# GpSimd no longer splits weights, and a list scheduler gets new durations: a two-block transformer on one Trainium2 core

## The chip, the cores and the metric

The kernel runs on one core of one Trainium2 chip. The metric is the device time of one execution in microseconds; three executions are timed, and a profiled one gives the trace.

## The reference

The input is one sequence of 256 tokens of width 1024. Two blocks follow one another, with two layers each, all in float32.

- A layer of the first block is `x + 0.5*rmsnorm(swiglu(rmsnorm(x)))` (hidden width 2816), then `x + rmsnorm(token_mixing(rmsnorm(x)))`, then a second swiglu of the same kind. The mixing holds three kinds of attention (banded with a relative bias, differential, stick-breaking) and an output projection.
- A layer of the second block is `x + merged @ w_out`, where `merged` is a gated sum of three branches (sparse attention over compressed, selected and windowed keys; chunked gated linear attention; attention into 256 memory tokens), then `x + relu(rmsnorm(x) @ w_up)**2 @ w_down` with hidden width 4096.

Two formulas matter below: `rmsnorm(x, g) = x * rsqrt(mean(x*x) + eps) * g`, and the gated linear attention's decay, which the kernel builds by products with a running state (its "scan").

## The kernel before, in words

**Weights.** All weights are cut on the host into 636 "halves" of 128x1024 float32 (512 KB). `loads` brings them in order through SP's DMA queue into 3 raw buffers (`raw`). Each is split into a rounded part and a rest: `splits` writes the first (`hl<-raw`, a cast on ScalarE), and the second is `raw - first` (`hl<-raw,hl`). A matrix product is then three passes on TensorE (first by first, first by rest, rest by first), summed in PSUM. The ring of split weights (`hl`) has 6 places. The rest is computed by `lows` on VectorE, in one 128x1024 piece (two of 128x512 while `rush` is set, in a handover), or by `pooled` on GpSimd, in four pieces of 128x256. `pooled` runs only if `POOLED` is true; it takes the second weight in the line, or in a handover the first.

**Stages.** `ffn1`, `mix`, `ffn2` for layer 0 and 1, then `hyb`, `mlp` for layer 0 and 1. In each, TensorE goes through the weights in order. The 256 tokens are two row tiles, t = 0 and t = 1.

**Handover.** At the end of a stage `finish` does the last products tile by tile, and `residual` and `norm` make the next stage's input: ScalarE squares and sums (`scr<-b`), VectorE multiplies by the gain (`scr<-b,scr`), `rstd` takes the inverse root (VectorE adds, `small<-small`, and GpSimd raises to the power -0.5, `small<-small,mhalf`), VectorE adds to the residual (`x<-scr,small,x`, two of 128x512). Then the same again for the next norm, and `turn_half` scales (`scr<-x,small,scr`, two halves), TensorE transposes (`b<-ident,scr`, four for a half), ScalarE casts (`hT<-b`) and VectorE subtracts (`hT<-b,hT`). `ws_first` then starts the next stage's first weights on the tile that is ready. In the first block "fill" matmuls (`m<-hl,hmem`, keys and values of the memory tokens for the second block, 24 for a weight) stand between these steps on TensorE. `gains` loads the gains by a broadcast DMA to 128 rows and scales them on GpSimd (128x1024).

**Order.** No order is written by hand. Every task (`loads`, `splits`, `lows`, `residual`, ...) is a generator that yields operations, and `Sched.run` emits, again and again, the operation that could start earliest by its own model of the engines (ties by priority; `SLACK` and `YIELD` hold back some background work). The model's durations come from `Engine.make` (VectorE, ScalarE, GpSimd, DMA), `mm` and `tr` (TensorE) and `matmul`, `when`, `issue`, which also decide when an engine is free. So a changed number there moves instructions on all engines. Each engine then works through its list in order and waits on semaphores. Since `issue` emits everything, nearly all rows of the trace have its line, L546.

A slot given to the ring or the raw buffers is reused in order:

```
            for o in range(0, 1024, 256):
                s = slice(o, o + 256)
                yield self.nc.gpsimd.tensor_sub(t[:, 1, s], raw[:, s], t[:, 0, s].bitcast(FT))
            self.raws.put(raw)
```

In the scan of a `hyb` stage GpSimd multiplies by constants (`scr<-scr,tC` of 128x128, 128x256 and 128x512), and TensorE then takes the results in small products (`b<-scr,scr`). GpSimd also does the powers of the head norms (`sts<-sts,mhalf`, 128x16 for the queries of the sparse attention).

Of the kernel before, what the change touches and what calls it, by code (L numbers as in the profile page):

```python
# [302 lines left out]
class Op:  # L303

    __slots__ = ("eng", "call", "args", "kw", "cost", "tail", "outs", "ins", "tab", "rdy", "stamp", "fn", "load",
                 "passes", "cols", "dep", "name")

    def __init__(self, eng, call, args, kw, cost, outs, ins, tail=0.0, tab=None, fn=None, load=0.0, passes=1, cols=0.0):
        self.eng, self.call, self.args, self.kw, self.cost, self.tail, self.tab = eng, call, args, kw, cost, tail, tab
        self.load, self.passes, self.cols = load, passes, cols  # L310
        self.outs = [r for r in map(region, outs) if r]
        self.ins = [r for r in map(region, ins) if r]
        self.rdy = self.stamp = self.dep = self.name = None
        self.fn = fn

# [31 lines left out]
class Engine:  # L347
# [5 lines left out]
    def __getattr__(self, fn):  # L353
# [3 lines left out]
        def make(*args, **kw):  # L357
# [8 lines left out]
            if "dma" in fn:  # L366
                size = max(_free(a) for a in aps if a.space != bass.MemoryType.DRAM) * 4 * 128
                return Op(e, real, args, kw, size / 360e3, outs, ins, 1.8, fn=fn)
            ps = any(a.space == bass.MemoryType.PSUM for a in outs + ins)
# [10 lines left out]
            else:  # L380
                k, b = 2.07, 0.157
                if kw.get("op") == OP.pow:
                    k, b = 167.0, 0.3
                elif fn == "tensor_scalar":
                    k, b = 0.85, 0.24 if ptr else 0.15
                elif fn == "tensor_copy":
                    k = 3.4
                elif fn == "memset":
                    k, b = 1.0, 0.0
# [17 lines left out]
class Sched:  # L407
# [5 lines left out]
    def __init__(self):  # L413
        self.t = {}
        self.acc = {}
        self.ver = {}
        self.table = None
        self.tasks = []
# [67 lines left out]
    def stream(self, s, cost, cols):  # L486
# [10 lines left out]
        return s  # L497

    def matmul(self, op):
        w = self.ready(op)  # L500
        for i in range(op.passes):
            ld = max(self.loader, w) + op.load
            self.loader = max(ld, self.t.get("pe", 0.0) + 0.002)
            if i == 0:
# [4 lines left out]
    def when(self, op):  # L509
        c = self.t.get(op.eng, 0.0)  # L510
        if op.eng == "pe":
            return max(c, max(self.loader, self.ready(op)) + op.load)
        s = max(c, self.ready(op))
        if op.tab and self.table not in op.tab and op.fn:
            s += 1.28 if op.eng == "act" else 0.0
        return s

    def issue(self, t):
# [5 lines left out]
        if op.eng == "sp":  # L524
            self.t["sp"] = s + 0.06
            d = max(self.t.get("dma", 0.0), s)
# [5 lines left out]
        else:  # L532
            e = s + op.cost
            self.t[op.eng] = e
        for regs, w in ((op.ins, False), (op.outs, True)):
            for n, ps, p0, p1, lo, hi in regs:
# [10 lines left out]
        if self.log is not None and r is not None:  # L547
            op.name = getattr(getattr(r, "ins", r), "name", None)
            self.log.append((op.name, op.eng, op.fn, s, e, op.cost, op.rdy, op.dep and op.dep.name, op.dep and op.dep.eng, t.gen.__name__))
        self.step(t)  # L550
# [58 lines left out]
class Prog:  # L609
# [52 lines left out]
    def mm(self, out, lhsT, rhs, start, stop, **kw):  # L662
        n, m = _free(rhs), _free(lhsT)
        wide = 2 if rhs.dtype == FT else 1
        return Op("pe", self.nc.tensor.matmul, (out,), dict(lhsT=lhsT, rhs=rhs, start=start, stop=stop, **kw),
                  wide * 0.4167e-3 * n, [out], [lhsT, rhs], fn="mm", load=0.836e-3 * m, passes=wide,
                  cols=wide * n * rhs.shape[0] / 128)

    def tr(self, out, in_, k=128):
        i = self.ident[:k, :k]  # L670
        return Op("pe", self.nc.tensor.transpose, (out, in_, i), {}, 0.8333e-3 * k, [out], [in_, i], fn="tr", load=0.107, cols=2 * k)

# [71 lines left out]

    POOLED = True
    rush = False
# [1451 lines left out]
```

## Time and profile before

| | us |
|---|---|
| median of 3 executions | 2017.01 |
| lowest, highest | 2014.21, 2018.1 |
| the profiled execution's own time | 2013.92 |
| its span, first to last instruction | 2012.0 |
| TensorE (PE) busy | 1963.7 (98%) |
| VectorE (DVE) busy | 1424.6 (71%) |
| ScalarE (ACT) busy | 1203.0 (60%) |
| GpSimd (POOL) busy | 267.9 (13%) |

The span is a little shorter than the time, which also holds what lies before the first and after the last instruction. Busy means that an instruction of the engine was under way; matmuls are pipelined, so a busy TensorE need not be at its peak. The granted clock (PEclk, a share of 2.4 GHz) has the mean 0.993 over the span. PEld is TensorE's weight load, which runs beside its matmuls.

### The profile page before, as it was taken

To read this page: it belongs to the slowest core of one execution; us is meant where nothing else is said; L and a number is where in the kernel's file an instruction comes from. 1 tells how busy PE (TensorE), PEld (TensorE's weight loads), DVE (VectorE), ACT (ScalarE), POOL (GpSimd) and SP (SyncE) were. 2 spreads that over 40 slices of the span, in tenths; PEclk is the share of its full clock that TensorE was granted. 3 is DMA by queue.
4 is the path that set the end of the run, shared out by engine and by line. 5 is a ranking of instruction groups with operands and counts; after the bars stand their busy time and mean duration, and the time that the engine had idled before them with its cause. 6 is when DMAs were issued, how large, how long until landed. Compare 5 with 4: busy or idle time off the path is not lost. (4 is left out here: it accounts for less than half of the span.)

```text
span 2012.0 us, 31884 instructions
## 1 busy us (share of the span) xinstructions
PE 1963.7 (98%) x11942; PEld 1724.9 (86%) x11942; DVE 1424.6 (71%) x2525; ACT 1203.0 (60%) x2328; POOL 267.9 (13%) x317
## 2 busy tenths in 40 slices
PE   8999999999999999999999999999999999999999
PEld 7888878888888888888889889988888988998887
DVE  6666897666676678876668778676666787766665
ACT  6655785655565568765556657655455656745553
POOL 1000302000200030020003132320001222420000
PEclk9999999999999999999999999999999999999999
DMA  6656344655665644555565544345555544345553
GB/s 218 228 189 209 112 159 163 212 188 189 206 202 189 205 161 150 178 171 190 189 210 186 173 144 152 115 163 185 197 197 186 170 147 147 116 149 186 189 191 123
DMA packets 100561, 353.77 MB, mean 176 GB/s; under 512 B 12435, under 2 KB 13493, under 8 KB 100406
## 3 DMA queue, kind: packets, MB, share of 16 engines
q1 hardware_dynamic: 100406, 351.74, 52.6%
q8 instruction: 93, 1.52, 0.3%
q14 instruction: 62, 0.51, 0.1%
HBM read 350.64 MB, written 1.05 MB: 175 GB/s over the span
## 5 line engine op out<-in xcount | busy, mean ns | idle before, releaser
L546 PE MATMUL m<-hT,hl 128*128 128x256 f32 (+1 forms) x5856 | 975.5, 322 | 8.6 <-DVE hT L546 7.0
L546 PEld LDWEIGHTS m<-hT,hl 128*128 128x128 f32 x5856 | 854.2, 189 | 103.6 <-DVE hT L546 9.2
L546 ACT CAST hl<-raw 128x1024 fp32r<-128x1024 f32 (+1 forms) x690 | 671.6, 983 | 379.1 <-PE b L546 139.0
L546 DVE TENSOR_TENSOR hl<-raw,hl 128x1024 fp32r<-128x1024 f32 (+1 forms) x641 | 755.8, 1183 | 201.2 <-ACT hl L546 197.3
L546 PE MATMUL b<-hl,chunk 128*128 128x512 f32 x2208 | 516.9, 390 | 0.0
L546 PEld LDWEIGHTS b<-hl,chunk 128*128 128x128 f32 x2208 | 408.8, 188 | 81.8 <-issue 0.7
L546 DVE TENSOR_TENSOR mid<-m,lo 128x256 f32<-128x256 f32 x256 | 108.3, 423 | 220.6 <-ACT lo L546 220.3
L546 PE MATMUL b<-hl,hT 128*128 128x512 f32 (+2 forms) x672 | 148.9, 370 | 1.0 <-DVE hT L546 1.0
L546 ACT CAST chunk<-mid 128x256 fp32r<-128x256 f32 x152 | 61.8, 407 | 120.9 <-DVE mid L546 120.5
L546 POOL TENSOR_SCALAR scr<-scr 128x1024 f32<-128x1024 f32 x17 | 21.4, 1258 | 826.5 <-DMA scr<-ffn_post_g 451.4
L546 PEld LDWEIGHTS b<-hl,hT 128*128 128x128 f32 x672 | 116.0, 188 | 16.5 <-DVE hT L546 1.3
L546 POOL TENSOR_TENSOR hl<-raw,hl 128x256 fp32r<-128x256 f32 x104 | 100.0, 987 | 190.1 <-ACT hl L546 152.8
L546 ACT COPY lo<-m 128x256 f32<-128x256 f32 x256 | 95.0, 371 | 22.2 <-PE m L546 21.3
L546 PE MATMUL b<-ident,scr 128*128 128x128 f32 (+2 forms) x458 | 79.7, 288 | 20.1 <-DVE scr L546 13.0
L546 PEld LDWEIGHTS b<-ident,scr 128*128 128x128 f32 (+2 forms) x458 | 55.0, 146 | 35.9 <-DVE scr L546 18.9
L546 PE MATMUL m<-chunk,hl 128*128 128x256 f32 x576 | 81.3, 290 | 0.0
L546 PEld LDWEIGHTS m<-chunk,hl 128*128 128x128 f32 x576 | 74.5, 195 | 1.7 <-ACT scr L546 0.7
L546 ACT ACTIVATE scr<-scr,sts 128x16 f32<-128x16 f32 (+2 forms) x152 | 62.7, 415 | 6.9 <-DVE sts L546 6.6
L546 DVE TENSOR_TENSOR chunk<-mid,chunk 128x256 fp32r<-128x256 f32 x152 | 65.2, 429 | 1.9 <-ACT chunk L546 1.7
L546 POOL TENSOR_SCALAR scr<-scr,sts 128x128 f32<-128x128 f32 (+2 forms) x96 | 58.1, 623 | 61.1 <-DVE sts L546 43.7
L546 ACT COPY scr<-b 16x16 f32<-16x16 f32 (+6 forms) x148 | 35.2, 238 | 36.8 <-PE b L546 29.4
L546 ACT ACTIVATE mid<-mid 128x256 f32<-128x256 f32 x88 | 36.7, 417 | 34.0 <-DVE mid L546 34.0
(205 smaller groups left out, 1598.4 us busy)
## 6 DMA issues: line engine op xcount, KB each, us to landing
raw<-w SPq DMA_DIRECT2D x636, 512.0 KB, 3.4
scr<-mem SPq DMA_DIRECT2D x4, 512.0 KB, 6.4
scr<-ffn_post_g SPq DMA_DIRECT2D x4, 512.0 KB, 5.2
bias<-bias SPq DMA_DIRECT2D x6, 256.0 KB, 3.6
scr<-ffn_pre_g SPq DMA_DIRECT2D x3, 512.0 KB, 5.1
scr<-mem_norm SPq DMA_DIRECT2D x2, 512.0 KB, 4.7
scr<-mix_pre_g SPq DMA_DIRECT2D x2, 512.0 KB, 4.5
bias<-alibi SPq DMA_DIRECT2D x4, 256.0 KB, 5.9
```

The lines of the kernel that those rows point to most:

```text
L546: r = op.call(*op.args, **op.kw) if op.call is not None else None
```

## The change

`POOLED` becomes `False`, so `pooled` is never started and `lows` on VectorE does all the rests. The scheduler's model changes:

- TensorE: a matmul column, the weight load, a step and a transpose get other durations; an operation carries the row count of its moving operand (`mode`), and going from one count to another costs `SWITCH`.
- GpSimd's power gets a longer duration.
- Operations of GpSimd (but for memset) and operations of VectorE with two inputs of more than one column in SBUF are marked `shared`; a shared operation of one engine does not start, in the model, while one of the other runs.
- A DMA takes longer to land (longest for a broadcast), and SP needs 0.46 for an issue.

```diff
-    def __init__(self, eng, call, args, kw, cost, outs, ins, tail=0.0, tab=None, fn=None, load=0.0, passes=1, cols=0.0):
+    def __init__(self, eng, call, args, kw, cost, outs, ins, tail=0.0, tab=None, fn=None, load=0.0, passes=1, cols=0.0,
+                 mode=None):
...
-        self.fn = fn
+        self.fn, self.mode = fn, mode
+        self.shared = eng == "pool" and fn != "memset" or eng == "dve" and sum(
+            not r[1] and r[5] - r[4] > 1 for r in self.ins) > 1
...
-                return Op(e, real, args, kw, size / 360e3, outs, ins, 1.8, fn=fn)
+                wide = any(a.space == bass.MemoryType.DRAM and a.ap[0][0] == 0 for a in aps)
+                return Op(e, real, args, kw, size / 360e3, outs, ins, 3.4 if wide else 1.9, fn=fn)
...
-                    k, b = 167.0, 0.3
+                    k, b = 200.0, 0.55
...
+    SWITCH = 0.195
+    STEP = 0.0105
+
     def matmul(self, op):
         w = self.ready(op)
+        if op.mode != self.mode:
+            if self.mode is not None:
+                w = max(w, self.t.get("pe", 0.0) + self.SWITCH - op.load)
+            self.mode = op.mode
         for i in range(op.passes):
             ld = max(self.loader, w) + op.load
-            self.loader = max(ld, self.t.get("pe", 0.0) + 0.002)
+            self.loader = max(ld, self.t.get("pe", 0.0) + self.STEP)
...
         if op.eng == "pe":
-            return max(c, max(self.loader, self.ready(op)) + op.load)
+            back = self.SWITCH if self.mode not in (None, 128) and op.mode != self.mode else 0.0
+            return max(c + back, max(self.loader, self.ready(op)) + op.load)
         s = max(c, self.ready(op))
+        if op.shared:
+            s = max(s, self.t.get("lock" + op.eng, 0.0))
...
         if op.eng == "sp":
-            self.t["sp"] = s + 0.06
+            self.t["sp"] = s + 0.46
...
             self.t[op.eng] = e
+            if op.shared:
+                self.t["lockdve" if op.eng == "pool" else "lockpool"] = e
...
-                  wide * 0.4167e-3 * n, [out], [lhsT, rhs], fn="mm", load=0.836e-3 * m, passes=wide,
-                  cols=wide * n * rhs.shape[0] / 128)
+                  wide * 0.4227e-3 * n, [out], [lhsT, rhs], fn="mm", load=0.836e-3 * m + 0.011, passes=wide,
+                  cols=wide * n * rhs.shape[0] / 128, mode=rhs.shape[0])
...
-        return Op("pe", self.nc.tensor.transpose, (out, in_, i), {}, 0.8333e-3 * k, [out], [in_, i], fn="tr", load=0.107, cols=2 * k)
+        return Op("pe", self.nc.tensor.transpose, (out, in_, i), {}, 0.098, [out], [in_, i], fn="tr", load=0.109, cols=2 * k,
+                  mode=128 if k > 64 else self.sch.mode)
...
-    POOLED = True
+    POOLED = False
```

What is computed stays the same. TensorE has the same 11620 matmul instructions. GpSimd's 104 pieces (26 weights) become weights of VectorE: its pieces of 128x1024 go from 579 to 602, those of 128x512 from 62 to 68. Along TensorE's list the moving operand's row count changes 95 times, 111 before. On SP's queue the gain broadcasts stand behind more weight loads, mostly by 1 or 2 (`mix_post_g` of layer 0 behind 104, 103 before; `mix_pre_g` behind 65, 63 before).

First place: GpSimd in the handover from ffn1 to mix of layer 0 (around 200 us in the trace). `small_108` and `small_109` belong to the two row tiles, `sts_78` to the fill. Before:

```order
L546 TENSOR_TENSOR small_108<-small_108,mhalf 128x1 x2
L546 TENSOR_TENSOR small_109<-small_109,mhalf 128x1
L546 TENSOR_TENSOR hl_100<-raw_93,hl_100 128x256 x4
L546 TENSOR_TENSOR hl_101<-raw_95,hl_101 128x256 x2
L546 TENSOR_TENSOR small_109<-small_109,mhalf 128x1
L546 TENSOR_TENSOR hl_101<-raw_95,hl_101 128x256 x2
L546 TENSOR_TENSOR sts_78<-sts_78,mhalf 128x4
L546 TENSOR_TENSOR hl_97<-raw_94,hl_97 128x256 x4
```

and of the change:

```order
L562 TENSOR_SCALAR scr_77<-scr_77 128x1024
L562 TENSOR_SCALAR scr_73<-scr_73 128x1024
L562 TENSOR_TENSOR small_108<-small_108,mhalf 128x1 x2
L562 TENSOR_TENSOR small_109<-small_109,mhalf 128x1 x2
L562 TENSOR_TENSOR sts_78<-sts_78,mhalf 128x4
L562 MEMSET bias_142 64x2x64
```

Six pieces of two weights stood between the two powers of the second row tile, and six more behind them; now nothing does.

Second place: GpSimd in the scan of the hybrid stage of layer 0 (around 1180 us). The names with `tC` are the scan's products, `sts_82` with 128x16 is the power of the query norm. Before:

```order
L546 TENSOR_TENSOR sts_81<-sts_81,mhalf 15x2
L546 TENSOR_TENSOR sts_80<-sts_80,mhalf 128x2x2
L546 MEMSET scr_75 128x2x2x128
L546 TENSOR_TENSOR hl_97<-raw_94,hl_97 128x256
L546 TENSOR_TENSOR sts_82<-sts_82,mhalf 128x16
L546 TENSOR_TENSOR scr_75<-scr_77,tC 128x128
L546 TENSOR_TENSOR scr_77<-scr_77,tC 128x256
L546 TENSOR_TENSOR scr_77<-scr_77,tC 128x512
L546 TENSOR_TENSOR hl_97<-raw_94,hl_97 128x256 x3
```

and of the change:

```order
L562 TENSOR_TENSOR sts_80<-sts_80,mhalf 128x2x2
L562 MEMSET scr_72 128x2x2x128
L562 TENSOR_TENSOR sts_81<-sts_81,mhalf 15x2
L562 TENSOR_TENSOR scr_72<-scr_76,tC 128x128
L562 TENSOR_TENSOR scr_76<-scr_76,tC 128x256
L562 TENSOR_TENSOR scr_76<-scr_76,tC 128x512
L562 TENSOR_TENSOR sts_82<-sts_82,mhalf 128x16
L562 TENSOR_TENSOR scr_76<-scr_76,tC 128x256
```

The power of the query norm went from ahead of the three products to behind them.

Third place: VectorE in the handover from mix to ffn2 of layer 0 (around 340 us). `small_111` is the second row tile's, `mk` and `sts_79` are the fill's. Before:

```order
L546 SCALAR_TENSOR_TENSOR x<-scr_77,small_111,x 128x512 x2
L546 TENSOR_TENSOR hT<-b_68,hT 128x4x128
L546 TENSOR_TENSOR hT<-b_67,hT 128x4x128
L546 TENSOR_SCALAR small_111<-small_111 128x1
L546 TENSOR_TENSOR hl_98<-raw_95,hl_98 128x512
L546 SCALAR_TENSOR_TENSOR scr_76<-x,small_111,scr_73 128x512 x2
L546 TENSOR_TENSOR scr_72<-mk 128x512
```

and of the change:

```order
L562 SCALAR_TENSOR_TENSOR x<-scr_77,small_111,x 128x512 x2
L562 SCALAR_TENSOR_TENSOR scr_74<-x,small_110,scr_73 128x512 x2
L562 TENSOR_SCALAR small_111<-small_111 128x1
L562 TENSOR_TENSOR scr_72<-mk 128x512
L562 TENSOR_TENSOR hT<-b_67,hT 128x4x128
L562 TENSOR_REDUCE sts_79<-scr_72 128x4
L562 TENSOR_TENSOR hT<-b_65,hT 128x4x128
L562 SCALAR_TENSOR_TENSOR scr_76<-x,small_111,scr_73 128x512 x2
```

The second tile's scaling moved behind the square of `mk`, two subtractions for hT and a reduction. On TensorE, all 48 fill matmuls of this handover now stand ahead of its 16 transposes, which follow one another.

## Rows read from the trace of the kernel before

**Rows 1.** Windows view by stage: TensorE, weight load, VectorE, ScalarE, GpSimd busy, clock, DMA

```profile
200.00:225.00 25.00, 21.36 (x157) 19.65 (x156) 20.88 (x34) 15.12 (x35) 16.03 (x17) 1.00 0.31 110
...
335.00:352.00 17.00, 14.93 (x118) 14.05 (x117) 16.18 (x24) 9.90 (x21) 11.39 (x12) 1.00 0.35 115
352.00:530.00 178.00, 178.00 (x955) 153.39 (x954) 112.59 (x158) 102.54 (x163) 2.92 (x3) 1.00 0.61 202
...
sum 2012.00, PE 1963.74 PEld 1724.92 DVE 1424.57 ACT 1203.03 POOL 267.88; mean PE 70.13 PEld 61.60 DVE 50.88 ACT 42.97 POOL 9.57
```

**Rows 2.** Waits of TensorE: waited for, us in total, times, longest

```profile
PE b L546 <- DVE scr L546: 13.0, 20, 1.5
PE b L546 <- POOL scr L546: 10.9, 6, 3.5
PE m L546 <- DVE hT L546: 7.0, 9, 1.2
PE b L546 <- ACT hl L546: 3.9, 1, 3.9
```

**Rows 3.** Timeline, handover ffn1 to mix: start, duration, instruction, idle time before it

```profile
202.18 1.41 DVE L546 SCALAR_TENSOR_TENSOR x<-scr,small,x 128x512 f32<-128x512 f32 x2 [0.67 <-POOL small L546]
...
207.12 6.19 POOL L546 TENSOR_TENSOR hl<-raw,hl 128x256 fp32r<-128x256 f32 x6
207.32 2.38 DVE L546 SCALAR_TENSOR_TENSOR x<-scr,small,x 128x512 f32<-128x512 f32 x2
...
210.82 0.20 DVE L546 TENSOR_SCALAR small<-small 128x1 f32<-128x1 f32 x1
...
213.28 0.54 POOL L546 TENSOR_TENSOR small<-small,mhalf 128x1 f32<-128x1 f32 x1
...
213.85 2.34 DVE L546 SCALAR_TENSOR_TENSOR scr<-x,small,scr 128x512 f32<-128x512 f32 x2 [1.14 <-POOL small L546]
...
215.11 0.66 PE L546 MATMUL b<-ident,scr 128*128 128x128 f32 x4 [1.48 <-DVE scr L546]
```

**Rows 4.** Groups by form, weight splitting on GpSimd and VectorE: busy, mean ns, idle before

```profile
L546 POOL TENSOR_TENSOR hl<-raw,hl 128x256 fp32r<-128x256 f32 x104 | 100.0, 987 | 190.1 <-ACT hl L546 152.8 <-DVE hl L546 37.1
...
L546 DVE TENSOR_TENSOR hl<-raw,hl 128x1024 fp32r<-128x1024 f32 x579 | 709.6, 1229 | 194.2 <-ACT hl L546 192.7 <-PE b L546 0.8
```

**Rows 5.** Timeline, scan of the hybrid stage of layer 0

```profile
1180.70 3.80 POOL L546 TENSOR_TENSOR sts<-sts,mhalf 128x16 f32<-128x16 f32 x1
...
1184.47 7.68 POOL L546 TENSOR_TENSOR scr<-scr,tC 128x128 f32<-128x128 f32 x3
...
1192.20 1.50 PE L546 MATMUL b<-scr,scr 64*128 64x128 f32 x16 [3.52 <-POOL scr L546]
1192.92 0.59 PEld L546 LDWEIGHTS b<-scr,scr 64*16 64x16 f32 x14 [0.22 <-issue]
```

**Rows 6.** Windows view, stretches at half clock (columns as in rows 1)

```profile
743.80:747.20 3.40, 3.40 (x17) 3.40 (x18) 3.19 (x8) 2.22 (x5) 2.52 (x2) 0.50 0.44 154
...
1662.00:1668.80 6.80, 6.69 (x42) 5.77 (x43) 2.22 (x10) 1.32 (x8) 2.10 (x4) 0.50 0.49 172
1829.30:1832.70 3.40, 3.40 (x17) 3.40 (x18) 3.08 (x5) 1.18 (x2) 0.00 (x0) 0.50 0.69 195
```

**Rows 7.** Timeline, start

```profile
11.20 3.76 POOL L546 TENSOR_TENSOR hl<-raw,hl 128x256 fp32r<-128x256 f32 x4 [1.83 <-ACT hl L546]
```

**Rows 8.** Timeline, handover mix to ffn2 of layer 0

```profile
325.29 1.39 POOL L546 TENSOR_SCALAR scr<-scr 128x1024 f32<-128x1024 f32 x1 [25.56 <-DMA scr<-mix_post_g]
...
328.30 0.69 DVE L546 TENSOR_TENSOR scr<-b,scr 128x512 f32<-128x512 f32 x1 [1.07 <-ACT scr L546]
...
341.16 1.27 DVE L546 TENSOR_TENSOR hT<-b,hT 128x512 fp32r<-128x512 f32 x2
...
345.86 1.22 DVE L546 TENSOR_TENSOR scr<-mk 128x512 f32<-128x512 f32 x1
...
348.15 0.67 DVE L546 TENSOR_REDUCE sts<-scr 128x4 f32<-128x512 f32 x1
```

More of the change, by code (lines that the diff above doesn't have):

```diff
@@ L305 @@
     __slots__ = ("eng", "call", "args", "kw", "cost", "tail", "outs", "ins", "tab", "rdy", "stamp", "fn", "load",
-                 "passes", "cols", "dep", "name")
-    def __init__(self, eng, call, args, kw, cost, outs, ins, tail=0.0, tab=None, fn=None, load=0.0, passes=1, cols=0.0):
+                 "passes", "cols", "dep", "name", "mode", "shared")
+    def __init__(self, eng, call, args, kw, cost, outs, ins, tail=0.0, tab=None, fn=None, load=0.0, passes=1, cols=0.0,
+                 mode=None):
         self.eng, self.call, self.args, self.kw, self.cost, self.tail, self.tab = eng, call, args, kw, cost, tail, tab
@@ L416, in __init__ @@
         self.ver = {}
-        self.table = None
+        self.table = self.mode = None
         self.tasks = []
@@ L548, in issue @@
             op.name = getattr(getattr(r, "ins", r), "name", None)
-            self.log.append((op.name, op.eng, op.fn, s, e, op.cost, op.rdy, op.dep and op.dep.name, op.dep and op.dep.eng, t.gen.__name__))
+            self.log.append((op.name, op.eng, op.fn, s, e, op.cost, op.rdy, op.dep and op.dep.name, op.dep and op.dep.eng, t.gen.__name__, op.passes))
         self.step(t)
```

## The prediction

> **What bounds the kernel now.** I read the sum row of the windows view first. Of a span of 2012.0 us TensorE is busy 1963.74, so it is idle 48.3; VectorE is busy 1424.57 and GpSimd 267.88 [rows 1]. No engine but TensorE can set the time, and the number of matmuls does not change, so the change can win only idle time of TensorE and time in which it ran at half clock. In the body of a stage there is neither: from 352 to 530 us TensorE is busy 178 of 178 us while VectorE does 112.59 [rows 1]. The idle time lies where one stage hands the residual to the next: 25 - 21.36 = 3.64 us from 200 to 225 us, 17 - 14.93 = 2.07 from 335 to 352. VectorE there is nearly full, 20.88 of 25 and 16.18 of 17 [rows 1].
>
> The table of waits of TensorE says on what: transposes that wait for the normalised residual (DVE scr, 13.0 us in 20 waits), matmuls that wait for an operand written by GpSimd (POOL scr, 10.9 in 6), matmuls that wait for the transposed activation (DVE hT, 7.0 in 9), and one of 3.9 for a weight at the start [rows 2].
>
> Then I looked at what stands behind such a wait. From 200 us on, GpSimd splits weights for 6.19 us without a break (207.12, six pieces). VectorE's pair of instructions `x<-scr,small,x` takes 1.41 us alone at 202.18 and 2.38 beside those pieces at 207.32. The variance of the second row tile is ready at 211.02 (210.82 + 0.20), but GpSimd is still splitting and starts its power at 213.28; `scr<-x,small,scr` then takes 2.34 beside more pieces, and the transposes at 215.11 have waited 1.48 us [rows 3]. So splitting on GpSimd hurts the handover twice: it stands ahead of the power, and it slows VectorE. The Trainium skill ("SBUF — State Buffer", section "SBUF: two separate sides") calls the port pair of VectorE and GpSimd an exclusive lock, which a VectorE instruction with two SBUF inputs needs against a GpSimd one that reads SBUF. The trace agrees in direction: 2.38 against 1.41 for two instructions.
>
> **The change, part by part.** The sum is made against the profiled execution, 2013.92 us; the median of the runs, 2017.01, is 3.1 higher, and that is added at the end.
>
> *No splitting on GpSimd.* Its 104 pieces (26 weights, 100.0 us of GpSimd, mean 987 ns) go; VectorE takes 26 whole weights more, 26 x 1.229 = 32 us [rows 4], and stands at 1456 of 2012 us, 72%. Cost 0: in the bodies 65 of 178 us are free. In the handovers the cover is thin, but there it is returned: the two pairs at 207.32 and 213.85 give back 0.97 + 0.93 = 1.9 us [rows 3], about what one and a half weights cost. If it is not returned, the split weight itself comes late; that is in the second rival.
>
> *Transposes* (13.0 us): in the handover at 200 us the chain gets shorter by 2.26 us (power at 211.0 instead of 213.28), 0.97 and the slowdown of the first half of the last pair, about 0.45, together 3.7 against waits of 1.48 and some tenths. The same pattern stands in the other handovers. I take -9; ends 0 and -13.
>
> *Matmuls on hT* (7.0): they follow the transposes but also wait for VectorE's own subtraction, which now has weights beside it. -2; ends 0 and -7.
>
> *The decay scan of the hybrid stages* (two of the POOL scr waits are 3.52 us each). GpSimd before did a power of 128x16 from 1180.70 for 3.80 us, then three products (7.68 us), and TensorE waited 3.52 for the last, until 1192.20 [rows 5]. Now the 128x16 power stands behind the three products (second pair of orders above). That moves them up by up to 3.8 us, and the wait goes: -7 for two; ends 0 and -10.9. What is late next is the query head norm that needs that power, on VectorE; nothing on TensorE needs it before the scan is over.
>
> *Half clock.* After some of these waits the granted clock is 0.50: from 743.8 to 747.2 (first), from 1662.0 to 1668.8 (one of the two longest, TensorE busy 6.69), from 1829.3 to 1832.7 (last); there are five behind handovers and scans [rows 6]. Half of the busy time in them is lost: 1.7 in each of the three short ones, about 3.1 in each of the two long, 11.3 in all. It comes back only where the idle time ahead shrinks enough, which no row tells. I take not quite half, -5; ends 0 and -11.3.
>
> *Start.* The fourth weight waits for a raw buffer that GpSimd's pieces free at 14.96 (11.20 + 3.76) [rows 7]; TensorE waits 3.9 for it [rows 2]. Now VectorE frees the buffer, right after its first half of hT, by an estimate up to 3 us earlier, but does one more weight in the same stretch (1.2). -2; ends 0 and -3.9.
>
> *Row-count switches of TensorE.* The scheduler now prices a change between operands of 128, 64 and 30 rows, and there are 95 instead of 111. At one such place the weight load shows 0.22 us of "issue" in which it waits for nothing [rows 5]. 16 x 0.22 = 3.5 at most; many lie inside longer waits: -2; ends 0 and -3.5.
>
> *Gains.* The broadcasts of the post gains and next gains stand behind 1 or 2 more weight loads on SP's queue; a weight takes 2012 / 636 = 3.2 us on average. In the handover at 325 us the gain is scaled by 326.68 and first used at 328.30 [rows 8], so 1.6 us are spare and one load more makes that product 1.6 late; the second product of that tile sets the chain and is not delayed. Cost 0; ends 0 and +3.2 for the two places.
>
> *Handover mix to ffn2 of layer 0.* In the third order above, VectorE's `scr<-x,small_111,scr` for the second row tile now stands behind the square of `mk`, two hT subtractions and a reduction: 1.22 + 1.27 + 0.67 [rows 8], and 0.70 for its first half. All 48 fill matmuls stand ahead of the first transposes, so nothing is left to cover it. The copy of `mk` takes another 0.6 after the fill, the transposes of the first tile (twice 0.66) run beside it: 4.5 - 1.3 = 3.2, with the hops between engines about +3.5. Ends +2.5 and, if the clock falls, +5.2.
>
> *New waits.* Eight handovers and two scans are reordered. If each opens one wait of the mean size 13.0 / 20 = 0.65 it is 6.5, if none does 0: +3.3.
>
> Sum: -9 - 2 - 7 - 5 - 2 - 2 + 3.5 + 3.3 = -20.2, so 1993.7 in a profiled execution, **1997 us** as a median (-1.0%).
>
> **The rivals.**
> 1. *Only the removal pays.* The scheduler's new numbers move the order about without gain: the scans keep a wait of 3 us because their products still run beside VectorE, clock stretches stay, and what is left is half of the transposes' 13.0 (-6.5), the start (-2), the hT waits (-2) and the one handover made worse (+3.5): -7, 2010 us, with a reach of 2006 to 2013. For it: the reordered products are still slowed by VectorE. Against it: the scan's 3.8 us power is plainly ahead in the one order and behind in the other.
> 2. *Slower: VectorE becomes the bound of each handover.* It was 95% busy in one and 84% in another [rows 1]. It takes 2 to 4 weights more in each, in order, so that the normalisation of the second row tile stands behind subtractions, as in the third order above. If every handover idles as that one would (3.5, and 1.7 of half clock) in place of about 2.3 now, eight of them lose 8 x 2.9 = 23 us, less start, scans and switches (-11): +12, 2029 us; the point from which it decides is a loss of more than 11 / 8 = 1.4 us per handover. Against it: in seven of the eight the new order shows no such pile-up. The Trainium skill has a rule on this side ("Perfetto Trace Analysis", section "Optimizing Scalar/DVE Operations"): with VectorE saturated, giving work to ScalarE or even GpSimd may make sense. The same paragraph warns that the two share a port. By the first half this rival holds; the trace agrees with the second half, by the 2.38 against 1.41 [rows 3].
> 3. *Nothing to measure.* Half of rival 2 against half of the gains: 2013 to 2021. A measurement of this kernel tells about 0.2%, 4 us, from no change.
>
> **How the numbers follow.** Forecast 0.60, with a range of its own of 1984 to 2006; rival 1 0.20; rival 3 0.10; rival 2 0.10. Faster by over 0.2% is the first two with a little lost at the edge: 0.80; same 0.10; slower 0.10. The low end takes the scans, transposes and clock near their far ends (-35): 1982. The high end, 2014, takes in rival 1; above it lie rivals 2 and most of 3, below 1982 very little.
>
> **What would show it.** GpSimd's busy time falls by about 100 us, to 165 to 175; VectorE's rises by less than 32, since the pairs at 207.32 and 213.85 [rows 3] fall to about 1.41. The waits on DVE scr fall under 5 us, those on POOL scr under 5, and the row of 3.52 is gone. The wait at the start is 1 to 2. At the handover mix to ffn2 of layer 0 one wait of some 3.5 us on DVE scr stands. The forecast is wrong if TensorE is idle for more than 40 us (rival 1) or if new waits on DVE scr or hT add to more than 20 (rival 2).

## The result: 2034.45 us, 0.9% slower, and the profile after

The changed kernel takes 2034.45 us (median of 4, 2029.76 to 2036.74) against 2016.88 before: a ratio of 1.0088, with a 95% interval of 1.0075 to 1.0101. 1997 was forecast, faster. The profiled execution took 2036.23 us, its span is 2034.4.

The page's first part, of the changed kernel (its line for "nearly all rows" is L562):

```profile
PE 1978.5 (97%) x11942; PEld 1733.1 (85%) x11942; DVE 1425.8 (70%) x2554; ACT 1200.1 (59%) x2320; POOL 142.9 (7%) x213
```

GpSimd fell by 125 us, more than its 100 us of pieces, since its products (`scr<-scr,tC`, 30.2 to 23.7) and scalings (`scr<-scr,sts`, 59.8 to 40.9) run faster too; its powers as a whole hardly changed. VectorE rose by only 1.2 us. TensorE is now idle 2034.4 - 1978.5 = 55.9 us, 7.6 more than before [rows 1]. Much of the rest of the loss is clock. The view of the cores gives its mean:

```profile
core 0: 2034.4 us, clock 0.987
```

Before, it was 0.993. In the trace the clock is at half for 51.2 us of the span, 29.2 before; half of that is lost, 25.6 and 14.6 us. So of the 22.4 us of span about 11 are half clock and 7.6 are idle time; the rest, some 4 us, these views do not split. That is the profiled execution alone: the other three had a mean clock of 0.990 to 0.992, and the one at 0.992 still took 2029.76 us, so half clock is only a part of the loss.

The waits of TensorE in the changed kernel, which answer to [rows 2]:

```profile
PE b L562 <- DVE scr L562: 19.8, 17, 3.0
PE m L562 <- DVE hT L562: 7.1, 6, 1.9
PE m L562 <- DVE mid L562: 5.6, 10, 1.2
PE b L562 <- DVE hl L562: 4.2, 2, 2.9
...
PE b L562 <- ACT hl L562: 0.8, 2, 0.5
PE b L562 <- POOL scr L562: 0.8, 1, 0.8
```

The waits that the change was to remove are gone: POOL scr from 10.9 to 0.8, the start (ACT hl) from 3.9 to 0.8. But DVE scr rose from 13.0 to 19.8, waits on `mid` from 0.7 to 5.6, and those on late weights (DVE hl, 4.2) are new. Nearly all the added waiting is on VectorE, whose busy time hardly grew. So it is not its load but the order of the work that got worse: that of VectorE's list, of TensorE's own, or of both.

Where that happened is seen by laying the two profiled runs side by side at the moments at which TensorE has done the same share of its matmul columns. The table is worked out so from the start times of all matmuls; a plus is time lost against the kernel before. The last column is an experiment of below, `pow_wait`.

| stretch, us of before | changed kernel | `pow_wait` |
|---|---|---|
| 0 to 110, start and first stage | +1.8 | +0.3 |
| 202 to 227, handover ffn1 to mix, layer 0 | -1.9 | -3.9 |
| 227 to 329, inside mix, layer 0 | +4.8 | +4.2 |
| 329 to 407, handover mix to ffn2, layer 0 | +4.1 | -0.9 |
| 518 to 538, handover ffn2 to ffn1 | -1.8 | -1.5 |
| 726 to 751, handover ffn1 to mix, layer 1 | -1.7 | -3.6 |
| 751 to 851, inside mix, layer 1 | +6.7 | +4.9 |
| 1059 to 1081, handover ffn2 to hyb | -2.5 | -2.2 |
| 1081 to 1167, start of hyb, layer 0 | +5.3 | +1.6 |
| 1167 to 1218, scan, layer 0 | +8.8 | -4.0 |
| 1218 to 1343, rest of hyb, layer 0 | -4.1 | -0.4 |
| 1641 to 1693, scan, layer 1 | +4.9 | -1.6 |
| 1693 to 1800, rest of hyb, layer 1 | -3.3 | -2.7 |

The handovers out of ffn1 and ffn2 did get shorter. The timeline of the one at 200 us shows why:

```profile
206.60 0.55 POOL L562 TENSOR_TENSOR small<-small,mhalf 128x1 f32<-128x1 f32 x1 [2.69 <-DVE small L562]
...
207.61 1.41 DVE L562 SCALAR_TENSOR_TENSOR scr<-x,small,scr 128x512 f32<-128x512 f32 x2
...
208.93 1.41 DVE L562 SCALAR_TENSOR_TENSOR x<-scr,small,x 128x512 f32<-128x512 f32 x2
...
212.02 0.55 POOL L562 TENSOR_TENSOR small<-small,mhalf 128x1 f32<-128x1 f32 x1 [3.26 <-DVE small L562]
```

The pairs at 207.61 and 208.93 take 1.41 us, as forecast (2.34 and 2.38 in [rows 3]), and no power waits behind pieces of weights.

The loss in the scan of layer 0 is seen in the windows view (columns as in [rows 1]):

```profile
1206.00:1209.60 3.60, 1.59 (x10) 1.06 (x8) 3.60 (x10) 1.98 (x4) 0.00 (x0) 1.00 0.00 0
1209.60:1213.00 3.40, 1.10 (x4) 0.88 (x5) 3.37 (x5) 0.22 (x1) 2.06 (x2) 0.50 0.00 0
...
1226.70:1230.10 3.40, 3.40 (x18) 3.40 (x18) 3.21 (x13) 1.32 (x3) 0.00 (x0) 0.50 0.81 266
1230.10:1235.00 4.90, 4.90 (x44) 4.90 (x44) 4.33 (x8) 3.99 (x12) 0.00 (x0) 1.00 0.60 216
```

The clock is at half from 1209.6 to 1230.1 us, six such windows in a row (first and last shown). Ahead of it, from 1206.0 to 1209.6, TensorE was busy 1.59 of 3.60 us while VectorE was busy throughout. The timeline of that place:

```profile
1201.19 2.90 POOL L562 TENSOR_TENSOR sts<-sts,mhalf 128x16 f32<-128x16 f32 x1 [4.28 <-DVE sts L562]
...
1202.55 0.40 DVE L562 TENSOR_TENSOR scr<-scr 30x256 f32<-30x256 f32 x1
...
1204.95 0.31 DVE L562 COPY_PREDICATED scr<-pred,b 128x128 f32<-128x128 uint8 x1 [2.00 <-ACT scr L562]
1205.16 1.22 DVE L562 TENSOR_TENSOR tA<-tA,sts 128x1024 f32<-128x1024 f32 x1
...
1206.49 1.09 PE L562 MATMUL b<-dec,sp 128*128 128x512 f32 x4
...
1208.09 0.27 DVE L562 TENSOR_SCALAR scr<-scr 30x256 f32<-30x256 f32 x1
...
1210.42 0.41 PE L562 MATMUL b<-ident,scr 30*128 30x30 f32 x2 [2.83 <-DVE scr L562]
...
1212.32 1.22 PE L562 MATMUL b<-scr,tC 64*128 64x256 f32 x2 [1.48 <-DVE scr L562]
```

Follow `scr<-scr 30x256` on VectorE, a small chain of the compressed keys. Its square is done at 1202.95, inside GpSimd's power of 2.90 us. The next step needs nothing but that square, but stands on VectorE's list behind the selections of the scan (`COPY_PREDICATED`, one of which waits 2.00 us for ScalarE) and the product that needs the power (1205.16). It runs at 1208.09. TensorE has the chain's transposes next on its own list, is done with what stands ahead of them at 1207.58 (1206.49 + 1.09) and waits 2.83 us; the clock falls within this wait, at 1209.6. A wait of 1.48 us for the scan's next product follows at half clock.

### The profile page after: what moved, and what is told of

The parts are those of the page before. It is cut to its first block, busy times and chain, and to the rows that moved or that the text cites. A ratio compares the mean times of both kernels' runs of the same rounds, so it can differ in the third digit from the quotient of the medians.

```text
span 2034.4 us, 31744 instructions
## 1 busy us (share of the span) xinstructions
PE 1978.5 (97%) x11942; PEld 1733.1 (85%) x11942; DVE 1425.8 (70%) x2554; ACT 1200.1 (59%) x2320; POOL 142.9 (7%) x213
## 4 chain that ended last, share of the span: by engine, by line
PE 73%; DVE 10%; DMA 7%; ACT 7%; issue 2%; POOL 0%; SPq 0%; ACTq 0%; DVEq 0%; POOLq 0%
PE m L562 39%; PE b L562 34%; DMA raw<-w 7%; DVE hl L562 3%; DVE scr L562 3%; ACT scr L562 3%; ACT hl L562 2%; ACT kst L562 1%; DVE mid L562 1%; DVE sts L562 0%; DVE hT L562 0%; DVE tA L562 0%; DMA scr<-pred 0%; ACT lo L562 0%; ACT qk L562 0%
## 5 line engine op out<-in xcount | busy, mean ns | idle before, releaser
L562 PE MATMUL m<-hT,hl 128*128 128x256 f32 (+1 forms) x5856 | 972.3, 322 | 15.4 <-DVE hT L562 7.1
L562 PEld LDWEIGHTS m<-hT,hl 128*128 128x128 f32 x5856 | 853.9, 190 | 109.9 <-DVE mid L562 8.6
L562 DVE TENSOR_TENSOR hl<-raw,hl 128x1024 fp32r<-128x1024 f32 (+1 forms) x670 | 779.2, 1168 | 208.0 <-ACT hl L562 200.8
L562 ACT CAST hl<-raw 128x1024 fp32r<-128x1024 f32 (+1 forms) x682 | 671.3, 993 | 408.8 <-PE b L562 136.3
L562 PE MATMUL b<-hl,chunk 128*128 128x512 f32 x2208 | 518.3, 391 | 0.0
L562 PEld LDWEIGHTS b<-hl,chunk 128*128 128x128 f32 x2208 | 408.9, 188 | 82.5 <-issue 1.4
L562 DVE TENSOR_TENSOR mid<-m,lo 128x256 f32<-128x256 f32 x256 | 108.5, 424 | 216.2 <-ACT lo L562 215.6
L562 PE MATMUL b<-hl,hT 128*128 128x512 f32 (+2 forms) x672 | 151.3, 372 | 4.6 <-DVE hl L562 4.2
L562 ACT CAST chunk<-mid 128x256 fp32r<-128x256 f32 x152 | 61.8, 407 | 127.4 <-DVE mid L562 127.4
L562 PEld LDWEIGHTS b<-hl,hT 128*128 128x128 f32 x672 | 116.5, 189 | 21.7 <-DVE hl L562 5.1
L562 ACT COPY lo<-m 128x256 f32<-128x256 f32 x256 | 94.6, 370 | 13.9 <-PE m L562 13.1
L562 PE MATMUL b<-ident,scr 128*128 128x128 f32 (+3 forms) x458 | 80.8, 294 | 19.7 <-DVE scr L562 16.8
L562 POOL TENSOR_SCALAR scr<-scr 128x1024 f32<-128x1024 f32 x17 | 21.9, 1286 | 966.9 <-DMA scr<-ffn_post_g 609.5
L562 PEld LDWEIGHTS b<-ident,scr 128*128 128x128 f32 (+3 forms) x458 | 56.4, 149 | 35.5 <-DVE scr L562 25.2
L562 PE MATMUL m<-chunk,hl 128*128 128x256 f32 x576 | 84.6, 298 | 0.2
L562 PEld LDWEIGHTS m<-chunk,hl 128*128 128x128 f32 x576 | 77.0, 202 | 1.7 <-issue 0.9
L562 ACT ACTIVATE scr<-scr,sts 128x16 f32<-128x16 f32 (+2 forms) x152 | 62.7, 415 | 10.1 <-DVE sts L562 9.7
L562 DVE TENSOR_TENSOR chunk<-mid,chunk 128x256 fp32r<-128x256 f32 x152 | 65.5, 431 | 3.9 <-ACT chunk L562 3.8
L562 ACT ACTIVATE mid<-mid 128x256 f32<-128x256 f32 x88 | 36.7, 417 | 38.1 <-DVE mid L562 38.0
L562 ACT COPY scr<-b 16x16 f32<-16x16 f32 (+6 forms) x148 | 35.0, 240 | 35.5 <-PE b L562 30.1
L562 PE MATMUL b<-hT,hl 128*128 128x256 f32 x384 | 50.2, 287 | 0.3 <-ACT hl L562 0.3
L562 PE MATMUL m<-hl,hmem 128*128 128x256 f32 x384 | 49.9, 284 | 0.0
```

Source lines behind the costliest of these rows:

```text
L562: r = op.call(*op.args, **op.kw) if op.call is not None else None
```

## The experiments

Each ran beside the kernel before on the same chip; a ratio is to those runs. There the kernel before took 2014.30 to 2015.82 us, 2016.88 beside the changed kernel, so differences between the times of two experiments are good to 2 or 3 us. "The lock" is the rule of the model by which a shared operation of GpSimd or VectorE does not start while one of the other runs.

**Which half of the change loses?** `pool_only` is the kernel before with this edit, `costs_only` the changed kernel with the reverse one:

```diff
-    POOLED = True
+    POOLED = False
```

> The kernel before with POOLED set to False and nothing else: VectorE does all the rests, the scheduler keeps its old durations. Theory A (VectorE as the sole splitter is the loss: it is late in the mixing stages and the handovers): 2028 to 2036 us, and in the mixing stage of layer 0 TensorE waits on VectorE as it does in the changed kernel. Theory B (the new durations are the loss, above all the price for a change of row count, which strings the small products of the scans together): 2005 to 2015 us, faster than before, with two handovers ffn1 to mix shorter by some 1.8 us each, the scans at full clock but for at most 7 us each.

> The changed kernel with POOLED back to True: GpSimd splits weights again, the new durations order the program. Theory A: 2010 to 2020 us, near the kernel before. Theory B: 2030 us or more, with a stretch at half clock of over 10 us in each of the two scans of the hybrid stages.

`pool_only` took 2012.36 us (0.9981, 0.9967 to 0.9996), `costs_only` 2066.72 (1.0256, 1.024 to 1.0271). Theory A is refuted: VectorE as the sole splitter is not slower. The new durations cost 51 us with splitting on GpSimd, and 22 us without (2034.45 against 2012.36). The two rows of `pool_only`'s waits that answer to [rows 2]:

```profile
PE b L546 <- POOL scr L546: 8.1, 6, 2.0
...
PE b L546 <- DVE scr L546: 3.2, 7, 0.9
```

The transposes' waits fell by 9.8 us, and TensorE's idle time by 7.8 (48.3 to 40.5), yet it gave only 3 us of time. Half clock took the rest: 51.2 us of the profiled span, 29.2 before, of which 37.4 lie in the two hybrid stages, where theory B allowed at most 7 us for each scan. Two of these stretches in the windows view:

```profile
1184.80:1195.00 10.20, 10.20 (x57) 8.64 (x57) 4.24 (x11) 1.60 (x10) 0.98 (x1) 0.50 0.32 104
1242.80:1253.00 10.20, 8.15 (x32) 6.67 (x33) 5.94 (x24) 5.16 (x19) 6.19 (x12) 0.50 0.22 76
```

So a hybrid stage can lose the clock without any of the new durations, too.

**Which of the new durations?** `no_switch` takes the row-count price out of both `matmul` and `when` (first edit), `no_lock` takes out the lock (second):

```diff
-        if op.mode != self.mode:
-            if self.mode is not None:
-                w = max(w, self.t.get("pe", 0.0) + self.SWITCH - op.load)
-            self.mode = op.mode
...
-            back = self.SWITCH if self.mode not in (None, 128) and op.mode != self.mode else 0.0
-            return max(c + back, max(self.loader, self.ready(op)) + op.load)
+            return max(c, max(self.loader, self.ready(op)) + op.load)
```

```diff
-        self.shared = eng == "pool" and fn != "memset" or eng == "dve" and sum(
-            not r[1] and r[5] - r[4] > 1 for r in self.ins) > 1
+        self.shared = False
```

> The changed kernel without the price for a change of row count on TensorE (both places taken out). Theory B in its narrow form (that price is the loss): the scan of the hybrid stage of layer 0 gets back about 10 of its 14 us, that of layer 1 some 4, so 2018 to 2024 us, and no stretch at half clock there is longer than 7 us. Theory A: within 4 us of the changed kernel, 2030 to 2038.

> The changed kernel without the lock between GpSimd and VectorE in the scheduler's model. If the lock holds back VectorE's work in the model and so puts it in a worse order: 5 to 10 us faster than the changed kernel, 2024 to 2030. Theories A and B (narrow) both say: within 4 us of the changed kernel, 2030 to 2038, with the long stretch at half clock still there. A third theory (any change of the scheduler's numbers shuffles the order, with an effect of either sign): a shift of 5 us or more either way, at places that have nothing to do with GpSimd.

`no_switch` took 2021.82 us (1.0037, 1.0024 to 1.005), `no_lock` 2016.41 (1.0, 0.999 to 1.001). Both gave back much. For the price it is what the narrow theory B said; for the lock it is 18 us, where its own expectation had 5 to 10 and theories A and B at most 4. `neither` takes both out:

> The changed kernel without the row-count price and without the lock; GpSimd splits nothing, the durations of matmul, transpose, power and DMA are the new ones. If the two are one cause (each alone tips the scans and the handovers mix to ffn2): about as the kernel without the lock, 2012 to 2020 us. If they add (12.6 us and 18 us back from 2034.45): near 2004 us. If the rest of the new durations is harmful too: over 2020.

2013.49 us (0.9985, 0.9974 to 0.9997): they do not add, so much of the harm of each needs the other. The other new durations (matmul, transpose, power, DMA) are, taken together, harmless: `pool_only`, with none of them, took 2012.36.

**Is it the choice or the clock of the model?** `switch_noback` takes the price out of `when` only, that is the last three lines of the first edit above.

> The changed kernel, with the row-count price kept in the model's clock of TensorE but taken out of the choice of the next operation. Theory (the price in the choice keeps TensorE on the small products and puts off the matmuls of the main stream): as the kernel without the price, 2018 to 2026 us, no stretch at half clock over 7 us in the scan of layer 0. Rival (the model's clock is what counts): within 4 us of the changed kernel, 2030 to 2038.

2033.65 us (1.0089, 1.0074 to 1.0104): no gain. My picture of a scheduler that keeps TensorE on small products to spare switches is refuted; the price in `matmul`, which shifts the model's times, does its harm without the one in `when`.

**Is the scheduler so touchy that any number moves the time?** `b_tick` is the kernel before with

```diff
-                    k, b = 167.0, 0.3
+                    k, b = 168.0, 0.3
```

> The kernel before with one number of the scheduler's model changed by next to nothing: a power takes 168 ns for an element, 167 before. If a change of the numbers acts by what it means: within 3 us of the kernel before, 2013 to 2019. If any change shuffles the order (theory C, the list scheduler is that sensitive): a shift of 5 us or more, of either sign.

2014.92 us (0.9994, 0.9984 to 1.0003). This is a weak test: but for TensorE's list and the place of one memset on VectorE, the lists came out the same, so it shows only that a number next to the old one does next to nothing. That larger changes move the time by the luck of an order remains a rival; the next experiments bear on it.

**Which operations does the lock get wrong?** `lock_nopow` leaves the lock and exempts the powers:

```diff
-        self.shared = eng == "pool" and fn != "memset" or eng == "dve" and sum(
+        self.shared = eng == "pool" and fn != "memset" and kw.get("op") != OP.pow or eng == "dve" and sum(
```

> The changed kernel, but GpSimd's powers are not marked shared, so that in the model they no longer hold back VectorE. Theory: the lock is wrong for the powers (in the trace of before a weight of VectorE takes its usual 1.21 us inside a power of 3.80 us), and that is its harm: 2014 to 2022 us, most of what the kernel without any lock gains. Rival: the harm is in the products and scalings that do slow VectorE, and the powers do not matter: 2030 to 2038.

2007.72 us (0.9963, 0.995 to 0.9976): 26.7 us faster than the changed kernel, and faster than with no lock at all. So the lock is useful for products and scalings, and harmful for powers. Two halves of it were then tried alone. `pow_hold` exempts powers from waiting (first edit), `pow_wait` from holding VectorE back (second edit):

```diff
-        if op.shared:
+        if op.shared and op.kw.get("op") != OP.pow:
             s = max(s, self.t.get("lock" + op.eng, 0.0))
...
-            if op.shared:
+            if op.shared and op.kw.get("op") != OP.pow:
                 self.t["lockdve" if op.eng == "pool" else "lockpool"] = e
```

> The changed kernel with one half of the powers' lock: in the model a power still holds back VectorE, but no longer waits for it. Theory D (the model lets VectorE stand still for the length of a power, which the chip does not do, so VectorE's list is put in a wrong order): 2028 to 2038 us, as the changed kernel, with the long stretches at half clock in the scans. Rival E (what harms is that the powers, which end each chain of a norm, are put off in the model until VectorE is free): 2006 to 2018.

> The other half: in the model a power waits for VectorE, but does not hold it back. Theory D: 2006 to 2018 us, near the kernel whose powers are out of the lock (2007.72), and no wait of 2.98 us on DVE scr in the handover mix to ffn2 of layer 0. Rival E: 2028 to 2038.

`pow_hold` took 2027.61 us (1.0055, 1.004 to 1.0071), `pow_wait` 2002.17 (0.9938, 0.9922 to 0.9954); both lie a little under the ranges of theory D and far from those of rival E. The harm is in the half by which VectorE stands still, in the model, for the length of a power. Both rows that show this of the chip are in traces. In the timeline of the kernel before, a product on VectorE that is under way when the power from 1180.70 to 1184.50 starts [rows 5], and a weight inside that power:

```profile
1180.54 1.21 DVE L546 TENSOR_TENSOR scr<-scr,tC 128x1024 f32<-128x1024 f32 x1
...
1182.47 1.21 DVE L546 TENSOR_TENSOR hl<-raw,hl 128x1024 fp32r<-128x1024 f32 x1
```

The weight takes 1.21 us, where its mean is 1.229 [rows 4]: this power takes nothing from VectorE. It is not alone: ten weights of 128x1024 in this trace lie mostly within a power, and their mean is 1.216 us, against 1.220 for the 515 with no work of GpSimd beside them. And in the timeline of `lock_nopow`, handover mix to ffn2 of layer 0, the powers at 339.84 and 341.16 beside VectorE's work:

```profile
339.68 0.68 DVE L562 TENSOR_TENSOR hl<-raw,hl 128x512 fp32r<-128x512 f32 x1
339.84 0.92 POOL L562 TENSOR_TENSOR small<-small,mhalf 128x1 f32<-128x1 f32 x1 [3.84 <-DVE small L562]
...
341.00 1.40 DVE L562 SCALAR_TENSOR_TENSOR scr<-x,small,scr 128x512 f32<-128x512 f32 x2
341.16 0.99 POOL L562 TENSOR_TENSOR small<-small,mhalf 128x1 f32<-128x1 f32 x1 [0.39 <-DVE small L562]
...
346.28 1.41 DVE L562 SCALAR_TENSOR_TENSOR scr<-x,small,scr 128x512 f32<-128x512 f32 x2
...
347.08 1.32 PE L562 MATMUL b<-ident,scr 128*128 128x128 f32 x8 [0.32 <-DVE scr L562]
```

They take 0.92 and 0.99 us, where one alone takes 0.55 (206.60 in the changed kernel), while VectorE's weight and pair take their usual 0.68 and 1.40. The contention goes one way: VectorE slows the power, and the rows say when. The weight under way at 339.84 ends at 340.36, and the power 0.40 us later (339.84 + 0.92), which reads as a wait for that end. `pow_wait`, the best of the locks, is the one that models just that. In its scan the small chain is no longer behind:

```profile
1180.58 2.89 POOL L562 TENSOR_TENSOR sts<-sts,mhalf 128x16 f32<-128x16 f32 x1 [0.25 <-DVE sts L562]
...
1180.85 0.41 DVE L562 TENSOR_TENSOR scr<-scr 30x256 f32<-30x256 f32 x1
...
1181.19 1.21 DVE L562 TENSOR_TENSOR hl<-raw,hl 128x1024 fp32r<-128x1024 f32 x1
...
1182.25 4.29 PE L562 MATMUL m<-hT,hl 128*128 128x256 f32 x34
1182.33 0.27 DVE L562 TENSOR_SCALAR scr<-scr 30x256 f32<-30x256 f32 x1
...
1182.53 1.21 DVE L562 TENSOR_TENSOR hl<-raw,hl 128x1024 fp32r<-128x1024 f32 x1
...
1184.00 0.29 DVE L562 COPY_PREDICATED scr<-pred,b 128x128 f32<-128x128 uint8 x1
...
1185.53 1.21 DVE L562 TENSOR_TENSOR tA<-tA,sts 128x1024 f32<-128x1024 f32 x1
...
1188.07 1.31 PE L562 MATMUL b<-scr,scr 64*128 64x128 f32 x20
...
1189.31 0.30 PE L562 MATMUL b<-ident,scr 30*128 30x30 f32 x2
```

The step that ran 5.1 us after the square in the changed kernel (1202.95 to 1208.09) runs 1.1 us after it (1181.26 to 1182.33), ahead of the selections, and TensorE's transposes at 1189.31 wait for nothing. That is not VectorE's list alone. From the end of the square to the transposes it takes 8.05 us here and 7.47 in the changed kernel; but here TensorE's own list, which the edit changes too, has enough work ahead of the transposes (from 1182.25 to 1189.38, when the matmuls of 1188.07 end). How the gain divides between the two lists was not tried. The mean clock:

```profile
core 0: 2000.7 us, clock 0.998
```

**Which powers?** `hold_norm` lets only the powers of 128x1 hold VectorE back, `hold_head` only the wider ones, by the width of the output (`== 1` for the first, `> 1` for the second); all powers wait for VectorE:

```diff
-            if op.shared:
+            if op.shared and (op.kw.get("op") != OP.pow or _free(op.args[0]) == 1):
                 self.t["lockdve" if op.eng == "pool" else "lockpool"] = e
```

> In the model only the powers of 128x1 (norms of the handovers) hold VectorE back; all powers wait for it. If the long powers of the head norms do the harm: 2002 to 2010 us. If the short ones do: 2022 to 2034, with the handovers mix to ffn2 and the mixing stages slow as in the changed kernel. If both share it: 2012 to 2020, the scans at full clock, the handovers slow.

> In the model only the powers of the head norms (more than one column) hold VectorE back. If they do the harm: 2022 to 2034 us, with a stretch at half clock of over 10 us in each scan. If the short ones do: 2002 to 2010. If both share it: 2012 to 2020, the scans slow, the handovers as with no hold at all.

2018.27 us (1.0016, 1.0007 to 1.0026) and 2014.19 (0.9992, 0.9983 to 1.0002), 16 and 12 above `pow_wait`; together they make 28 of the 32 us between it and the changed kernel (by the ratios, 0.8% and 0.5% of 1.5%). Both kinds share the harm, each at places of its own. `hold_norm` has the changed kernel's wait in the handover mix to ffn2 of layer 0, here in its timeline:

```profile
350.85 1.97 PE L562 MATMUL b<-ident,scr 128*128 128x128 f32 x8 [2.98 <-DVE scr L562]
```

`hold_head` has half clock in both scans, here in the windows view:

```profile
1192.70:1202.70 10.00, 7.91 (x45) 6.55 (x46) 7.96 (x17) 2.83 (x12) 2.06 (x2) 0.50 0.45 154
1663.70:1677.20 13.50, 11.60 (x60) 9.78 (x60) 10.00 (x24) 4.67 (x14) 3.22 (x3) 0.50 0.36 118
```

Neither has the other's: the transposes of that handover do not wait in `hold_head`, and the clock in the scans of `hold_norm` (1165 to 1215 and 1640 to 1685 us) is 1.00.

**What are the row-count price and the splitting worth with a right lock?** `nopow_noswitch` is `lock_nopow` with the edit of `no_switch`, `nopow_pooled` is `lock_nopow` with `POOLED` true, and `wait_noswitch` is `pow_wait` with the edit of `no_switch`:

> The kernel whose powers are out of the lock, without the row-count price. If the price is harmful by itself (12.6 us came back without it): 1995 to 2002 us. If it harmed only together with the powers' lock, or is right: 2005 to 2015, no faster than 2007.72.

> The kernel whose powers are out of the lock, with GpSimd splitting weights again. If splitting on GpSimd costs the chain of each handover some 3.7 us, as the prediction had it: 2020 to 2035 us, 12 us or more above 2007.72. If it is nearly free once the order is made with the right lock: within 5 us of 2007.72.

> The powers only wait for VectorE, and there is no row-count price. If the price is right (it tells the scheduler of a real cost): 2005 us or more, slower than 2002.2. If it is harmful: 1990 to 1999. If it is of no weight: within 3 us of 2002.2.

`nopow_noswitch` took 2004.99 us (0.9945, 0.993 to 0.996), 2.7 less than with the price; the intervals overlap, and it lies between its two expectations. `nopow_pooled` took 2016.84 (1.0004, 0.9991 to 1.0016): splitting on GpSimd costs 9.1 us under a right order, between the two expectations. `wait_noswitch` took 1996.29 (0.9904, 0.9888 to 0.9921), the fastest of all, 0.96% below the kernel before and 5.9 us below `pow_wait`. In its profiled execution the clock never fell enough to show in the mean:

```profile
core 0: 1992.9 us, clock 1.000
```

So the price, too, puts the program in a worse order, though it does what it was meant for: the row count changes 87 times along TensorE's list in `pow_wait`, 109 times in `wait_noswitch`. Whether its size is wrong (0.195 for every change of row count, where rows show 0.22 at single places [rows 5]) or only its effect on the order, was not tried.

These runs also bear on the rival that any change of the numbers moves the time by luck. Taking the powers out of the lock gains 26.7 us in the changed kernel, 16.8 without the row-count price (`no_switch` against `nopow_noswitch`) and 49.9 with splitting on GpSimd (`costs_only` against `nopow_pooled`): three different orders, one sign. Leaving the lock for the rest gains 8.7 us with the price (`no_lock` against `lock_nopow`) and 8.5 without (`neither` against `nopow_noswitch`). Differences of a few us between single orders are not told from luck.

## Why the prediction was wrong

It costed the new durations place by place, as reorderings that would on the whole do good, and had no term for an entry of the model that is wrong and so costs time wherever it is used. The entry by which a power holds VectorE back cost 32 us (2034.45 with it, 2002.17 without); the terms that it broke are the new waits (+3.3), the scan (-7) and the half clock (-5).

- **Removal of splitting**: right in kind. The pairs fell to 1.41, the power no longer waits, and VectorE's load rose by 1.2 us only. At its places the -9 for the transposes was about right: the four handovers out of ffn1 and ffn2 got 1.7 to 2.5 us shorter each, 7.9 together with all other terms in them, and, by the same reckoning, 12.7 in `pool_only`; in `lock_nopow` they are 7.8 us shorter than in `nopow_pooled`. As time of the whole it was worth 3 us by itself (`pool_only`, where half clock took the rest), 9 with the powers out of the lock, and 32 under the changed kernel's durations (`costs_only`).
- **Scan, -7**: the wait on POOL scr went as forecast, and the step failed all the same. I compared GpSimd's list alone. VectorE's list in the same place had been reordered too, by the power's hold (`hold_head` has the half clock there, `hold_norm` has not), and the scans lost 8.8 and 4.9 us, where `pow_wait` gains 4.0 and 1.6.
- **Half clock, -5**: wrong sign; about 11 us more were lost to it. In the scan shown, TensorE was waiting for VectorE when it fell. The removal alone had the same sign (`pool_only`), with none of the new entries in it; why is open.
- **Handover mix to ffn2 of layer 0, +3.5**: right. The order showed the pile-up, and the wait is there, 2.98 us, with the rows in the order that was read:

```profile
345.52 0.55 POOL L562 TENSOR_TENSOR small<-small,mhalf 128x1 f32<-128x1 f32 x1 [2.37 <-DVE small L562]
...
346.66 0.69 DVE L562 TENSOR_TENSOR scr<-mk 128x512 f32<-128x512 f32 x1 [1.22 <-ACT mk L562]
347.27 0.68 DVE L562 TENSOR_TENSOR hT<-b,hT 128x512 fp32r<-128x512 f32 x1
347.87 0.68 DVE L562 TENSOR_REDUCE sts<-scr 128x4 f32<-128x512 f32 x1
348.46 0.68 DVE L562 TENSOR_TENSOR hT<-b,hT 128x512 fp32r<-128x512 f32 x1
349.06 1.40 DVE L562 SCALAR_TENSOR_TENSOR scr<-x,small,scr 128x512 f32<-128x512 f32 x2
...
349.86 1.97 PE L562 MATMUL b<-ident,scr 128*128 128x128 f32 x8 [2.98 <-DVE scr L562]
```

The scaling runs at 349.06 although its power, begun at 345.52, took 0.55. In `lock_nopow` it comes ahead of the subtractions and the wait is 0.32. I read this place as an accident of one handover; it was the mark of the wrong entry, which holds VectorE's scaling back in the model after each power (`hold_norm` has the same wait of 2.98 us).

- **New waits, +3.3**: the step that failed most. The price of a reordered place was taken as one mean wait in ten handovers and scans. Inside the mixing stages alone, 4.8 and 6.7 us were lost, 5.3 at the start of the first hybrid stage. I had not looked there: that the body of a stage has no idle time was read off one ffn2 stage, while from 225 to 335 us, in mix, TensorE was busy 107.50 of 110 us before the change already.
- **Start, -2**: right as far as it went; at 25 us the changed kernel is 2.6 us ahead. But 4.3 us are lost from there to 110 us, where TensorE was never idle before and now is for 2.65 us; net +1.8.
- **Matmuls on hT, -2, and row-count switches, -2**: neither came. The waits on hT stayed (7.0 and 7.1), and the price that spares the switches costs time: 12.6 us in the changed kernel (`no_switch`), 5.9 in `pow_wait`.
- **Rival 2** had the sign and almost the size (2029), by another mechanism: VectorE is at 70%, not the bound; the work is in a wrong order. By the rule of the Trainium skill that rival leaned on ("Perfetto Trace Analysis", section "Optimizing Scalar/DVE Operations"), giving VectorE's work to GpSimd may help where VectorE is saturated; here it is at 71%, and it does not help (2016.84 with, 2007.72 without).
- **The exclusive lock** of the Trainium skill ("SBUF — State Buffer", section "SBUF: two separate sides") is not what these runs show for a power: the trace had the row that says so (1.21 us inside 3.80) before the prediction, and I quoted the rule without asking which GpSimd operations it holds for. That row, laid against the diff, which marks every operation of GpSimd but memset, pointed at the wrong entry, though not at its price.

What stays open: why the inside of the mixing stages loses 4 to 5 us in `pow_wait` too (about 2 in `pool_only`), how much of the harm is VectorE's list and how much TensorE's own, and how much of `wait_noswitch`'s lead is one good draw of an order.

## What to carry to other kernels

When a change edits the numbers by which a scheduler orders the work, check each new entry against a row of the trace that contradicts it, in both directions (does A slow B, does B slow A), before costing any place; one wrong hold cost more (32 us) than the whole change could win. Read the order of the engine that is waited for, at every stage that uses it, not only at the places that the change means to help. And an engine that is busy 70% of the time can still cost time by the order of the work: VectorE's load was the same (1425.8 and 1425.4 us) in the changed kernel and in `pow_wait`, 32 us apart.

## What the runs showed of the hardware

A power on GpSimd and two-input instructions of VectorE contend in one direction only: the power went from 0.55 to 0.92 and 0.99 us, VectorE stayed at 0.68 and 1.40. Subtractions on GpSimd, by contrast, slowed VectorE's pair from 1.41 to 2.38 [rows 3]. For the power it is the start that counts in the rows shown: that of 128x16 took 3.80 us where a product of VectorE (1180.54 to 1181.75) was under way when it started, and 2.89 in `pow_wait`, where two weights (1181.19 and 1182.53) began after it and ran within it.
